# Summing the modulation's eight row tiles on VectorE instead of TensorE

## The chip, the cores and the metric

One core of one Trainium2 chip runs the whole program in one launch. The metric is the device time of an execution in microseconds (us); lower is better. PE is TensorE, DVE is VectorE, ACT is ScalarE, POOL is GpSimd, SP is SyncE, which issues most of the loads.

## What is computed

Two transformer layers on 256 context and 256 sequence tokens with 1024 features, and then a second block. Each layer first makes its modulation: shifts, scales and gates, six vectors of 1024 for each of two conditioning vectors.

```python
mod = (silu_c @ lp["w_mod"] + lp["b_mod"])[:, None, :]
sh1, sc1, gt1, sh2, sc2, gt2 = jnp.split(mod, 6, axis=-1)
n_mod_c = 6 * d if update_ctx else 2 * d
modc = (silu_cc @ lp["w_mod"][:, :n_mod_c] + lp["b_mod"][:n_mod_c])[None, None, :]
...
x = x + gt1 * merge_branches(o_mla, o_gqa, o_four, proj[..., GATE_START:], lp)
x = x + gt2 * conv_ffn(modulate(x, lp["g_norm2"], sh2, sc2), lp)
```

`w_mod` is [1024, 6144] float32 in each layer. The last layer (`update_ctx` false) uses only the first 2048 columns of the context's modulation.

## The kernel before

Products of activations and weights are made of float32 operands split into two float32r parts. `wload` (L223) loads 128 x 1024 elements of a weight on SP's queue into one of four slots `wraw`; `wsplit` (L237) makes a piece of it: ACT casts the high part `whi` (L247), DVE subtracts it to get the low part `wlo` (L249), in four slots each; then PE runs three matmuls for each pair of tiles (`mm3`, L259 to L261). With 512 tokens a piece feeds 24 such matmuls. A product's sum is held in one of five PSUM banks (`acc`) until ACT or DVE has read it.

The modulation of the first layer's first group of 2048 columns is made at the start (`first_mod`). The five other groups (two of layer 0, three of layer 1) come from the class `Mod` in 40 steps of 128 rows by 2048 columns. A step loads 1 MB of `w_mod` into a slot `mraw` (L457; two slots in the first place, three in the second) and PE multiplies it with `cT`, the conditioning vectors as 32 columns (two are used, 30 are zero), by four matmuls of 512 columns (L459) that lie on four column tiles of the array, and sums over the eight steps of a group in the PSUM bank `po`. After the eighth step `close` copies `po` to SBUF (L474), transposes it (L393) and adds the bias (L477).

The steps are traced in two places. In layer 0's remaining branches, between attention and the product with `w_o`, `mod.step(4)` stands four times between a gate's product (four pieces) and a branch's product (two pieces); the branch's operand `bhl` is split by ACT and DVE too (L378, L379), its sums are multiplied by the gate and added up on DVE (L874, L890). In layer 0's FFN, `mod.step(3)` stands after each pair of hidden tiles: a pair is four tiles of `w_up` (four pieces), each convolved by ACT and two operations of DVE on the PSUM bank (L1154, L1157), multiplied (L1205) and split (`xh`, `xl`, L379); after every second pair comes the product with `w_down`, whose sums DVE adds to the residual (L1080). The residual's gate, `hgt`, and the second norm need layer 0's two groups; layer 1 needs the other three.

What order an engine runs its instructions in is settled when the program is built: the builder moves instructions of one engine past each other where their operands allow it. At run time each engine and each DMA queue takes its own instructions in that order, and a wait holds up all behind it.

Of the kernel before, what the change touches and what calls it, by code (L numbers as in the profile page):

```python
# [10 lines left out]
F32 = mybir.dt.float32  # L11
# [26 lines left out]
def constants():  # L38
# [19 lines left out]
    # bucket of the relative position k - 255, k = 0..511 (the last one is unused)  # L58
# [24 lines left out]
class Packed:  # L83
    """A matrix [K, N], stored part by part in the order in which the program loads them; each partition's share of
    a part [k * 128 rows, c columns] is one run of k * c elements."""
# [17 lines left out]
class View:  # L103
# [8 lines left out]
    def part(self):  # L112
        """The access pattern [128, k, c] of a part that is loaded once."""
        m, n = self.m, self.shape[0] * self.shape[1]
        pos, m.pos = m.pos, m.pos + n
        assert m.pos <= m.size
        m.parts.append((pos, self.r0, self.r1, self.c0, self.c1))
        return m.ap[pos : pos + n].rearrange("(p k c) -> p k c", p=P, c=self.shape[1])


def feature_major(a):
    """[.., k * 128] as [128, .., k]"""
    a = a.reshape(*a.shape[:-1], -1, P)
    return np.moveaxis(a, -1, 0)


def setup(nc, inputs):
    """Access patterns by name, and a function that gives the arrays once the program is there."""
# [8 lines left out]
    for n in MATS:  # L137
        A[n] = []
        for l in range(i[n].shape[0]):
            a = i[n][l]  # L140
            if n == "w_br_gqa":
                # heads in the order in which the attention pairs them: one of each key head
                a = a.reshape(2, 4, 64, D).swapaxes(0, 1).reshape(512, D)
            packs.append(Packed(nc, f"{n}_{l}_dram", a, SLACK.get(n, 0)))
            A[n].append(packs[-1].view())
    put("w_mod", i["w_mod"])
    # the first layer's first shift and scale, one half of the features after the other
# [25 lines left out]
def tile_kernel(ctx: ExitStack, tc: tile.TileContext, A, C, out):  # L173
# [21 lines left out]
    # instructions that others are queued behind  # L195
# [6 lines left out]
    # PSUM banks: products and scores, transposes, attention outputs and small sums  # L202
# [19 lines left out]
    RAW = 1024  # L222

    def wload(src):
        """src: a view [k*128, cols], at most RAW elements for each partition."""
# [10 lines left out]
    def wsplit(v, into=None):  # L236
        """Parts of a piece [128, k, c] of a loaded tile, at most 1024 elements; into: a tile [128, 2, 1024]."""  # L237
# [16 lines left out]
    def hold(n):  # L254
        """The next n pieces are split behind what has been traced with to_hilo: they are ready early and would go first."""
# [7 lines left out]
    def proj_fm_steps(w, c0, ncols, act, evict, T):  # L263
        """Feature-major product: evict(ct, psum[features, T]) for each tile of 128 columns of w; a step is a tile."""
# [21 lines left out]
    def fm_half(ws, act, os_, a, ks=range(KD), n=256):  # L286
        """As proj_fm for split tiles of 128 columns and the tokens from a, a half; to be finished for both halves before
        the products in os_ are read. A step is a tile."""
# [7 lines left out]
    def tm_half(ws, n, act, tts, evict, os_=None, k=0):  # L296
        """As proj_tm for split row tiles of one window, from k, and some of the tokens. A step is a split piece."""
# [13 lines left out]
    def halves_last(ws, act, evict):  # L311
        """As proj_fm for weights that stay, all products of 256 tokens before those of the others; ws(): their split
        parts in order; evict(ct, psum, first token). A step is a tile."""
# [18 lines left out]
    def beside(work, bg, skip=0):  # L332
        """Steps of work, with one of bg after each but the first ones."""
# [4 lines left out]
    def pipeline(units, fill=None, every=1):  # L338
        """Stage j of unit i is emitted beside stage 0 of unit i + j; fill: steps of other work in between."""
# [8 lines left out]
    def proj_tm_steps(w, c0, widths, act, tts, evict):  # L348
        """Token-major product: evict(tt, window, psum[tokens, width]); a step is a split piece of w."""
# [31 lines left out]
    def rsqrt_cols(ss, n, mul, eps, name):  # L381
        """(ss * mul + eps) ** -0.5 for a [128, n] tile of sums."""
# [6 lines left out]
    def transposed(src_tiles, dst_evict, rows=P):  # L389
        """PE transposes of up to four [128, c] blocks into one PSUM bank."""  # L390
# [5 lines left out]
    # ================================================================ block 1  # L396
    # the residual, feature-major: a list of tiles [128, tokens]; its slots hold gates between its uses
# [12 lines left out]
    # silu of the two conditioning vectors, feature-major, padded to a column tile of the array  # L410
# [6 lines left out]
    # parameters by feature  # L417
# [10 lines left out]
    def after(t, x):  # L428
        """What is loaded into t comes after x."""
# [3 lines left out]
    def load_par(l):  # L433
        small.dma_start(out=par[l]["all"], in_=A["par"][l])
        small.dma_start(out=rowbc[l]["all"], in_=A["rows"][l].partition_broadcast(P))
        # the attention scales go with the queries' gains
# [6 lines left out]
    class Mod:  # L443
        """Modulation columns in groups of 2048 for both conditioning vectors, four column tiles of the array at work.
        step() does one tile of 128 rows; finish() those that are left of a group."""

        def __init__(self, src, bufs, *groups):
            self.todo, self.o, self.src, self.bufs = [], None, src, bufs
            self.todo = [(l, g, k) for l, g in groups for k in range(KD)]

        def step(self, n=1):
            for _ in range(min(n, len(self.todo))):
                l, g, k = self.todo.pop(0)
                if k == 0:
                    self.o = psum([P, 512], tag="po")
                raw = self.src.tile([P, 2048], F32, tag="mraw", name="mraw", bufs=self.bufs)
                nc.sync.dma_start(out=raw, in_=A["w_mod"][l, k * P : (k + 1) * P, g * 2048 : (g + 1) * 2048])  # L457
                for j in range(4):
                    nc.tensor.matmul(  # L459
                        self.o[32 * j : 32 * j + 32, :], cT[:, k, :], raw[:, j * 512 : (j + 1) * 512], start=(k == 0), stop=(k == KD - 1)  # L460
                    )
                if k == KD - 1:
                    self.close(l, g)
# [4 lines left out]
        def slot(self):  # L468
            """A slot of the loads' ring for a split piece."""
# [18 lines left out]
    def first_mod(h, ks=range(KD)):  # L488
        """Shift and scale of the first norm for a half of the features, four column tiles of 256 columns."""
# [3 lines left out]
        for k in ks:  # L493
            # the split weights' slots are free yet
# [24 lines left out]
    class Squares:  # L519
        """Sums of squares over feature tiles: the last tile's stay apart."""  # L520
# [5 lines left out]
        def add(self, k, a, T):  # L526
            """Feature tile k of the residual, T tokens from a."""
# [12 lines left out]
        def columns(self, o, t0, t1):  # L540
            """Sums over all features, 128 tokens to a column."""
# [5 lines left out]
    # tokens: columns 0..255 are the context's, 256..511 the sequence's  # L547
    def norm_factor(acc, t0, t1, res, tag="acc"):
        """rsqrt of the mean square over features (acc: Squares), on all partitions, in PSUM; in steps."""
# [14 lines left out]
    def norm_steps(l, which, acc, a, scaled=False, ks=range(KD), rb=None):  # L564
        """The modulated norm of 256 tokens from a, in two parts; scaled: X has been multiplied by the norm's factor."""
# [36 lines left out]
    # the first layer's residual can be read again: the tiles take the norm's factor  # L602
# [7 lines left out]
    def rope_apply(x, nh, off, half, cs):  # L610
        """Rotate x[:, :, off:off+2*half] in place; cs: [128, 4*half] = cos, cos, -sin, sin."""
# [10 lines left out]
    def head_rstd(x, nh, dh):  # L622
        """rsqrt of the mean square over each head's dims; x: [128, nh, dh]."""
# [12 lines left out]
    def layer(l):  # L636
# [31 lines left out]
        # ---- products of the input that the attentions start from  # L668
# [50 lines left out]
        # the first weights stay in slots that are taken later, for the second half of the tokens  # L719
# [9 lines left out]
        if full:  # L729
            # half of the features after the other, as their shift and scale come  # L730
# [19 lines left out]
            # fills the time that the second half's norm takes  # L750
# [20 lines left out]
        # the residual waits in DRAM, the first layer's is the input  # L771
# [10 lines left out]
        def ev_qg(tt, wi, o):  # L782
            # [j, g, d]: the four queries of a group lie side by side over the two key heads
# [28 lines left out]
        # ---- the Fourier branch; its tiles lie where the latent heads will  # L812
# [42 lines left out]
        # ---- gates that are ready before their branches: work for the array between the attentions' steps  # L855
# [13 lines left out]
        def half_tanh(dst, o):  # L869
            """sigmoid(z) = (1 + tanh(z / 2)) / 2; the last factor goes with the residual's gate."""  # L870
# [12 lines left out]
        def branch_evict(bi, gs, ct0=0):  # L883
            """y = sum over branches of (1 + tanh) * (branch @ its matrix)"""
# [22 lines left out]
        # ---- latent attention's heads  # L907
# [62 lines left out]
        # ---- attention: a unit is two heads for 128 queries  # L970
        def unit(name, tt, i, heads):
# [4 lines left out]
            def a():  # L976
                st["p"] = []
                # two heads of 64 dims lie on two row tiles of the array
# [23 lines left out]
            def c():  # L1002
# [3 lines left out]
                # the two heads on two column tiles of the array  # L1006
# [34 lines left out]
        # ---- the branches that are left  # L1041
# [6 lines left out]
        for bi, n, wn in ((1, "gqa", "w_br_gqa"), (2, "mla", "w_br_mla"))[nb - 1 :]:  # L1048
            b = load_branch((mp if full else qk).tile([P, 2, 4, T], F32R, tag="bhl" if full else "KT", name="bhl"), n)
            for dq in range(2):  # L1050
# [8 lines left out]
                if not full:  # L1059
                    # the first pieces of w_up; the context's halves of the first norm are free  # L1060
# [6 lines left out]
        # the residual returns; in the second layer only the sequence's half is of use  # L1067
# [33 lines left out]
        else:  # L1101
            # the first products of w_up go ahead of the norm's factor, which multiplies them by token:
            # (x r A + B) w = r (x A) w + B w, B as one more column
# [32 lines left out]
        # ---- FFN  # L1136
# [11 lines left out]
        def conv(u, m, name):  # L1148
            """The depthwise taps over tokens for feature tile m; u: PSUM [128, T]."""
# [13 lines left out]
        # two tiles first for the first layer, two last for the second  # L1163
# [5 lines left out]
        def pair(m0):  # L1169
            av = []  # L1170
            if full and m0 == 0:
                # the first products start with the first half of the tokens
# [50 lines left out]
        # a group's second product comes after some of the next group's first ones: its operand is ready by then  # L1223
# [661 lines left out]
```

## Time and profile before

| | us |
|---|---|
| median of 3 runs (1899.38 to 1901.94) | 1900.52 |
| span of the profiled execution | 1896.8 |
| PE busy in it | 1841.1 |
| DVE busy in it | 1265.7 |
| ACT busy in it | 933.0 |

The profiled execution has no time of its own beside its span, from the first to the last instruction. The median is 3.7 us above that span, which is what lies around it if that execution took the median time. The granted TensorE clock is 0.993 of full speed on average. A busy PE is not PE at its peak: matmuls overlap in the records, so a group's busy time is to be read together with the starts of what follows.

### The profile page before, as it was taken

The numbers are of one execution on the slowest core, as the hardware profiler recorded it, in microseconds if no ns is written. First come the engines' busy times: TensorE is split into PE (matmuls) and PEld (weight loads), VectorE is DVE, ScalarE is ACT, GpSimd is POOL, SyncE is SP. The second block draws the span as 40 slices with busy tenths as digits, with TensorE's granted clock in tenths as the row PEclk, the third lists the DMA queues.
The fourth block names the chain that finished last, engine by engine and source line by source line (L and its number), as shares of the span: only waits on it lengthen the run. The fifth ranks groups of instructions, "written<-read, shape, count | busy, mean of one in ns | idle before, by whom it ended". The sixth has DMA issues, their size and how long they took to land.

```text
span 1896.8 us, 30401 instructions
## 1 busy us (share of the span) xinstructions
PE 1841.1 (97%) x11962; PEld 1555.0 (82%) x11962; DVE 1265.7 (67%) x2317; ACT 933.0 (49%) x1561; POOL 149.9 (8%) x149
## 2 busy tenths in 40 slices
PE   6999999999999999999999999999999999999998
PEld 4788666777797777778899977999999887799996
DVE  5657776434575555456577987688787768668776
ACT  3435454223343323323445554565556647477782
POOL 0303100200120000000121200010000000200010
PEclk9999999999999999999999999999999999999999
DMA  8322210666426545422344522545565446344442
GB/s 325 114 72 77 73 62 29 205 241 222 167 79 232 178 156 211 156 89 90 108 149 149 162 83 77 195 145 188 180 192 193 160 162 201 116 145 150 156 142 98
DMA packets 86319, 281.07 MB, mean 148 GB/s; under 512 B 9616, under 2 KB 24224, under 8 KB 80288
## 3 DMA queue, kind: packets, MB, share of 16 engines
q1 hardware_dynamic: 65376, 254.91, 39.5%
q10 hardware_dynamic: 18992, 19.40, 3.2%
q0 software_dynamic: 1808, 4.82, 0.9%
q8 instruction: 94, 1.54, 0.3%
q14 instruction: 49, 0.40, 0.1%
HBM read 272.26 MB, written 8.93 MB: 148 GB/s over the span
## 4 chain that ended last, share of the span: by engine, by line
PE 88%; DVE 4%; ACT 3%; DMA 2%; issue 2%; POOL 0%; SPq 0%; ACTq 0%; DVEq 0%; POOLq 0%
PE acc L259 25%; PE acc L261 24%; PE acc L260 24%; PE acc L981 3%; PE tp L393 3%; PE po L1009 2%; PE po L459 2%; DMA mraw<-w_mod_dram 1%; PE acc L1326 1%; DVE wlo L249 1%; PE po L1354 1%; ACT whi L247 1%; DVE m L1310 0%; ACT L1432 0%; DVE scc L1270 0%
## 5 line engine op out<-in xcount | busy, mean ns | idle before, releaser
L249 DVE TENSOR_TENSOR wlo<-wraw,whi 128x1024 fp32r<-128x1024 f32 (+3 forms) x364 | 436.9, 1203 | 241.4 <-ACT whi L247 238.0
L247 ACT CAST whi<-wraw 128x1024 fp32r<-128x1024 f32 (+3 forms) x364 | 373.1, 1030 | 442.0 <-PE acc L260 352.4
L261 PE MATMUL acc<-hh,wlo 128*128 128x256 f32 (+1 forms) x1184 | 399.4, 338 | 0.0
L260 PE MATMUL acc<-hl,whi 128*128 128x256 f32 (+1 forms) x1184 | 399.1, 338 | 0.0
L259 PE MATMUL acc<-hh,whi 128*128 128x256 f32 (+1 forms) x1184 | 399.1, 338 | 0.0
L259 PEld LDWEIGHTS acc<-hh,whi 128*128 128x128 f32 x1184 | 223.4, 189 | 32.2 <-issue 4.2
L260 PEld LDWEIGHTS acc<-hl,whi 128*128 128x128 f32 x1184 | 222.9, 188 | 26.5 <-issue 2.0
L261 PEld LDWEIGHTS acc<-hh,wlo 128*128 128x128 f32 x1184 | 223.1, 189 | 24.8 <-issue 0.3
L261 PE MATMUL acc<-xh,wlo 128*128 128x256 f32 (+1 forms) x336 | 111.3, 332 | 0.0
L260 PE MATMUL acc<-xl,whi 128*128 128x256 f32 (+1 forms) x336 | 111.2, 332 | 0.0
L259 PE MATMUL acc<-xh,whi 128*128 128x256 f32 (+1 forms) x336 | 110.9, 332 | 0.0
L1080 DVE SCALAR_TENSOR_TENSOR x<-acc,mod,x 128x256 f32<-128x256 f32 x144 | 65.0, 479 | 51.5 <-PE acc L261 50.8
L538 POOL TENSOR_TENSOR nacc<-nacc,nsq 128x256 f32<-128x256 f32 x30 | 32.3, 1076 | 700.5 <-ACT nsq L533 698.7
L259 PE MATMUL acc<-h4h,whi 128*128 128x256 f32 x288 | 82.5, 287 | 1.5 <-ACT g L1432 1.5
L261 PE MATMUL acc<-h4h,wlo 128*128 128x256 f32 x288 | 81.8, 285 | 0.0
L260 PE MATMUL acc<-h4l,whi 128*128 128x256 f32 x288 | 81.6, 284 | 0.0
L259 PEld LDWEIGHTS acc<-xh,whi 128*128 128x128 f32 x336 | 63.3, 189 | 11.9 <-issue 2.5
L986 ACT ACTIVATE p<-acc,negm 128x512 f32<-128x512 f32 (+1 forms) x96 | 58.9, 621 | 27.2 <-DVE negm L984 24.1
L386 POOL TENSOR_TENSOR hr_r<-hr_t,mhalf 128x4 f32<-128x4 f32 (+2 forms) x42 | 55.3, 1318 | 193.0 <-DVE hr_t L384 189.5
L261 PEld LDWEIGHTS acc<-xh,wlo 128*128 128x128 f32 x336 | 63.5, 189 | 6.3
L260 PEld LDWEIGHTS acc<-xl,whi 128*128 128x128 f32 x336 | 63.3, 188 | 6.0
L984 DVE TENSOR_REDUCE negm<-acc 128x1 f32<-128x512 f32 (+1 forms) x96 | 56.4, 596 | 13.7 <-PE acc L981 13.1
(456 smaller groups left out, 4154.2 us busy)
## 6 DMA issues: line engine op xcount, KB each, us to landing
wraw<-w_up_dram SPq DMA_DIRECT2D x84, 512.0 KB, 3.8
mraw<-w_mod_dram SPq DMA_DIRECT2D x40, 1024.0 KB, 6.4
wraw<-w_in_dram SPq DMA_DIRECT2D x74, 512.0 KB, 3.5
wraw<-w_in_c_dram SPq DMA_DIRECT2D x60, 512.0 KB, 3.3
wraw<-w_down_dram SPq DMA_DIRECT2D x44, 512.0 KB, 3.8
wraw<-w_in_ab_dram SPq DMA_DIRECT2D x41, 512.0 KB, 4.1
mraw<-w_mod_dram SPq DMA_DIRECT2D x16, 512.0 KB, 9.8
wraw<-w_out_ab_dram SPq DMA_DIRECT2D x12, 512.0 KB, 3.7
```

The lines of the kernel that those rows point to most:

```text
L247: nc.scalar.copy(out=w(hi), in_=v)
L249: nc.vector.tensor_tensor(out=w(lo), in0=v, in1=w(hi).bitcast(F32), op=ALU.subtract)
L259: nc.tensor.matmul(o, lh, rh, start=first, stop=False)
L260: nc.tensor.matmul(o, lh, rl, start=False, stop=False)
L261: last_ops["pe"] = nc.tensor.matmul(o, ll, rh, start=False, stop=last)
L386: last_ops["pow"] = nc.gpsimd.tensor_tensor(out=r[:, :n], in0=t[:, :n], in1=mhalf[:, :n], op=ALU.pow)
L393: last_ops["tp"] = nc.tensor.transpose(o[: s.shape[1], j * P : j * P + s.shape[0]], s, ident[: s.shape[0], : s.shape[0]])
L459: nc.tensor.matmul(self.o[32 * j : 32 * j + 32, :], cT[:, k, :], raw[:, j * 512 : (j + 1) * 512], start=(k == 0), stop=(k == KD - 1))
L981: nc.tensor.matmul(S, q, k[:, :nk], start=True, stop=True)
L984: nc.vector.tensor_reduce(out=m[:, 0:1], in_=S, axis=AX.X, op=ALU.max, negate=True)
L986: nc.scalar.activation(out=p[:, :nk], in_=S, func=AF.Exp, bias=m[:, 0:1], scale=1.0, accum_out=m[:, 1:2])
L1080: nc.vector.scalar_tensor_tensor(out=X[ct][:, a : a + 256], in0=o[:, a - t0 : a - t0 + 256], scalar=gate[:, ct, w : w + 1], in1=X[ct][:, a ...
```

## The change

A step no longer uses PE. For each conditioning vector `v` it multiplies the loaded tile by that vector's column of `cT`, one number for each partition, and adds it to an accumulator `macc` of 128 x 2048 in SBUF, in two halves of 1024: one `tensor_scalar` for a half in a group's first step, one `scalar_tensor_tensor` in the seven others, all on DVE. After the eighth step PE sums each accumulator over the partitions into `po`, by four matmuls whose stationary operand `pick` is 32 columns with ones in column `v` and zeros elsewhere. In layer 1's second and third groups only the sequence's vector is made. The accumulators take 16 KB more of each partition in both places. Comments were removed too; what stands in the diff is all else.

```diff
+    pick = const1("pick", [P, 2, 32])
+    nc.vector.memset(pick, 0.0)
+    for v in range(2):
+        nc.vector.memset(pick[:, v, v : v + 1], 1.0)
...
         def step(self, n=1):
             for _ in range(min(n, len(self.todo))):
                 l, g, k = self.todo.pop(0)
+                vs = range(1 if l and g else 2)
                 if k == 0:
-                    self.o = psum([P, 512], tag="po")
+                    self.acc = [self.src.tile([P, 2048], F32, tag=f"macc{v}", name="macc") for v in vs]
                 raw = self.src.tile([P, 2048], F32, tag="mraw", name="mraw", bufs=self.bufs)
                 nc.sync.dma_start(out=raw, in_=A["w_mod"][l, k * P : (k + 1) * P, g * 2048 : (g + 1) * 2048])
-                for j in range(4):
-                    nc.tensor.matmul(
-                        self.o[32 * j : 32 * j + 32, :], cT[:, k, :], raw[:, j * 512 : (j + 1) * 512], start=(k == 0), stop=(k == KD - 1)
-                    )
+                for v in vs:
+                    for s in (slice(0, 1024), slice(1024, 2048)):
+                        a, c = self.acc[v][:, s], cT[:, k, v : v + 1]
+                        if k == 0:
+                            nc.vector.tensor_scalar(out=a, in0=raw[:, s], scalar1=c, scalar2=None, op0=ALU.mult)
+                        else:
+                            nc.vector.scalar_tensor_tensor(out=a, in0=raw[:, s], scalar=c, in1=a, op0=ALU.mult, op1=ALU.add)
                 if k == KD - 1:
+                    o = psum([P, 512], tag="po")
+                    for v in vs:
+                        for j in range(4):
+                            nc.tensor.matmul(
+                                o[32 * j : 32 * j + 32, :], pick[:, v], self.acc[v][:, j * 512 : (j + 1) * 512], start=(v == 0), stop=(v == vs[-1])
+                            )
+                    self.o = o
                     self.close(l, g)
```

The builder moves other instructions with it. In the changed program line numbers below `Mod` are 18 higher (L1154 is L1172, L1205 is L1223, L874 is L892). Three places:

PE, at the end of the first gate's product in the branches (`hh` is the norm's output, `bhl` the branch's operand, `po` the bank of the modulation). Before, here after two steps:

```order
L261 MATMUL acc<-hh,wlo 128x512
L459 MATMUL po<-mraw,cT 32x512 x8
L259 MATMUL acc<-bhl,whi 128x512
L260 MATMUL acc<-bhl,whi 128x512
L261 MATMUL acc<-bhl,wlo 128x512
```

Now, where the first group ends, after the second gate's product:

```order
L261 MATMUL acc<-hh,wlo 128x512
L477 MATMUL po<-macc,pick 32x512 x2
L259 MATMUL acc<-bhl,whi 128x512
L260 MATMUL acc<-bhl,whi 128x512
L477 MATMUL po<-macc,pick 32x512 x2
L261 MATMUL acc<-bhl,wlo 128x512
L259 MATMUL acc<-bhl,whi 128x512
L260 MATMUL acc<-bhl,whi 128x512
```

No matmul of a step is left; a group's eight come in four pairs here, with matmuls of the branch between them.

DVE, from the last of some parameters' operations (`nq`) on, in the branches. Before:

```order
L1849 TENSOR_SCALAR nq<-omlb 128x12
L249 TENSOR_TENSOR wlo<-wraw,whi 128x1024
L379 TENSOR_TENSOR bhl<-braw,bhl 128x512
L249 TENSOR_TENSOR wlo<-wraw,whi 128x1024
L379 TENSOR_TENSOR bhl<-braw,bhl 128x512 x3
L249 TENSOR_TENSOR wlo<-wraw,whi 128x1024
L874 SCALAR_TENSOR_TENSOR gate<-gate,acc 128x512
L890 TENSOR_TENSOR gt_1339<-gt_1339,gate 128x512
L874 SCALAR_TENSOR_TENSOR gate<-gate,acc 128x512
L890 TENSOR_TENSOR gt_1340<-gt_1340,gate 128x512
```

Now:

```order
L1867 TENSOR_SCALAR nq<-omlb 128x12
L470 TENSOR_SCALAR macc<-mraw,cT 128x1024 x4
L472 SCALAR_TENSOR_TENSOR macc<-mraw,cT,macc 128x1024 x4
L249 TENSOR_TENSOR wlo<-wraw,whi 128x1024
L472 SCALAR_TENSOR_TENSOR macc<-mraw,cT,macc 128x1024 x7
L249 TENSOR_TENSOR wlo<-wraw,whi 128x1024
L379 TENSOR_TENSOR bhl<-braw,bhl 128x512
L472 SCALAR_TENSOR_TENSOR macc<-mraw,cT,macc 128x1024
L379 TENSOR_TENSOR bhl<-braw,bhl 128x512
L249 TENSOR_TENSOR wlo<-wraw,whi 128x1024
L379 TENSOR_TENSOR bhl<-braw,bhl 128x512 x2
L472 SCALAR_TENSOR_TENSOR macc<-mraw,cT,macc 128x1024 x7
```

The branch's operand was split beside the next two pieces; 15 operations of the modulation now stand ahead of its first split, and one more ahead of the second.

DVE in the FFN, from the first hidden tile's multiplication on (`cv` are convolved tiles, `xh` and `xl` the split hidden tile). Before:

```order
L1205 TENSOR_TENSOR cv<-cv 128x512
L1154 SCALAR_TENSOR_TENSOR cv<-acc,par_99,cv 128x2x255
L1157 SCALAR_TENSOR_TENSOR cv<-acc,par_99,cv 128x2x255
L379 TENSOR_TENSOR xl<-cv,xh 128x512
L1205 TENSOR_TENSOR cv<-cv 128x512
L379 TENSOR_TENSOR xl<-cv,xh 128x512
L249 TENSOR_TENSOR wlo<-wraw,whi 128x512
L1154 SCALAR_TENSOR_TENSOR cv<-acc,par_99,cv 128x2x255
```

Now:

```order
L1223 TENSOR_TENSOR cv<-cv 128x512
L470 TENSOR_SCALAR macc<-mraw,cT 128x1024 x4
L1172 SCALAR_TENSOR_TENSOR cv<-acc,par_103,cv 128x2x255
L379 TENSOR_TENSOR xl<-cv,xh 128x512
L472 SCALAR_TENSOR_TENSOR macc<-mraw,cT,macc 128x1024 x4
L1175 SCALAR_TENSOR_TENSOR cv<-acc,par_103,cv 128x2x255
L249 TENSOR_TENSOR wlo<-wraw,whi 128x512
L472 SCALAR_TENSOR_TENSOR macc<-mraw,cT,macc 128x1024
L1172 SCALAR_TENSOR_TENSOR cv<-acc,par_103,cv 128x2x255
L472 SCALAR_TENSOR_TENSOR macc<-mraw,cT,macc 128x1024 x3
L1223 TENSOR_TENSOR cv<-cv 128x512
L249 TENSOR_TENSOR wlo<-wraw,whi 128x512
```

The second hidden tile's multiplication came soon after the first's, with its split `xl` right behind it. Now twelve of the modulation's operations stand between the two multiplications, four more and three convolution operations between the second one and its split, and a tile's second convolution operation no longer follows its first at once.

## Rows read from the trace of the kernel before

**Rows 1.** The page's first part: busy time, share of the span, instructions

```profile
PE 1841.1 (97%) x11962; PEld 1555.0 (82%) x11962; DVE 1265.7 (67%) x2317; ACT 933.0 (49%) x1561; POOL 149.9 (8%) x149
```

**Rows 2.** The page's chain that ended last, by engine

```profile
PE 88%; DVE 4%; ACT 3%; DMA 2%; issue 2%; POOL 0%; SPq 0%; ACTq 0%; DVEq 0%; POOLq 0%
```

**Rows 3.** Stages by window: us, PE, PEld, DVE, ACT, POOL busy, PEclk, DMA share, GB/s

```profile
340.00:500.00 160.00, 157.89 (x755) 113.77 (x753) 59.95 (x90) 41.74 (x58) 10.67 (x21) 1.00 0.63 222
580.00:820.00 240.00, 240.00 (x1114) 176.94 (x1113) 130.03 (x183) 79.45 (x101) 0.00 (x0) 1.00 0.50 181
```

**Rows 4.** The same windows, line 459's instructions alone: us, PE, PEld, PEclk

```profile
340.00:500.00 160.00, 16.22 (x128) 2.93 (x128) 1.00 0.63 222
580.00:820.00 240.00, 25.17 (x192) 5.26 (x192) 1.00 0.50 181
```

**Rows 5.** PE in order of time: start, us, line, tiles, count, idle before

```profile
367.17 0.40 PE L261 MATMUL acc<-hh,wlo 128*128 128x512 f32 x1
367.50 1.93 PE L459 MATMUL po<-mraw,cT 128*32 128x512 f32 x16
369.35 0.50 PE L259 MATMUL acc<-bhl,whi 128*128 128x512 f32 x1
...
379.23 1.07 PE L459 MATMUL po<-mraw,cT 128*32 128x512 f32 x8 [1.45 <-DMA mraw<-w_mod_dram]
```

**Rows 6.** The chain that ended last, in order of time, FFN of layer 0

```profile
605.16 2.71 PE po L459 x24
...
615.06 0.97 PE po L459 x2
```

**Rows 7.** Tile mraw: time to landing of its loads

```profile
DMA to landing us min/median/max: 4.8/7.0/13.7
```

**Rows 8.** PE's waits, 340 to 830 us: total, times, longest

```profile
PE po L459 <- DMA mraw<-w_mod_dram: 2.1, 2, 1.4
PE acc L259 <- ACT whi L247: 1.7, 2, 1.3
```

**Rows 9.** DVE groups by form: count, busy us, mean ns

```profile
L249 DVE TENSOR_TENSOR wlo<-wraw,whi 128x1024 fp32r<-128x1024 f32 x347 | 424.6, 1227 | 227.8 <-ACT whi L247 224.7 <-PE tp L393 1.7 <-PE acc L261 0.2
...
L993 DVE TENSOR_SCALAR p<-p,negm 128x512 f32<-128x512 f32 x64 | 30.8, 482 | 1.5
...
L993 DVE TENSOR_SCALAR p<-p,negm 128x256 f32<-128x256 f32 x32 | 10.7, 346 | 0.2
...
L1769 DVE SCALAR_TENSOR_TENSOR ke<-g,ke 128x1024 f32<-128x1024 f32 x6 | 7.3, 1209 | 0.0
```

**Rows 10.** DVE in order of time, the branches and w_o

```profile
353.33 0.17 DVE L1849 TENSOR_SCALAR nq<-omlb 128x12 f32<-128x12 f32 x1
...
501.23 2.36 DVE L249 TENSOR_TENSOR wlo<-woraw,whi 128x1024 fp32r<-128x1024 f32 x2
```

**Rows 11.** DVE in order of time, the first pairs of the FFN

```profile
581.17 0.74 DVE L1154 SCALAR_TENSOR_TENSOR cv<-acc,par,cv 128x510 f32<-128x510 f32 x1
581.95 0.75 DVE L1157 SCALAR_TENSOR_TENSOR cv<-acc,par,cv 128x510 f32<-128x510 f32 x1
582.62 0.68 DVE L379 TENSOR_TENSOR xl<-cv,xh 128x512 fp32r<-128x512 f32 x1
583.21 0.69 DVE L1205 TENSOR_TENSOR cv<-cv 128x512 f32<-128x512 f32 x1
...
689.55 0.88 DVE L1080 SCALAR_TENSOR_TENSOR x<-acc,mod,x 128x256 f32<-128x256 f32 x2 [1.92 <-PE acc L261]
```

**Rows 12.** PE in order of time, where the second pair's products begin

```profile
579.34 0.39 PE L260 MATMUL acc<-hl,whi 128*128 128x512 f32 x1
579.57 0.39 PE L261 MATMUL acc<-hh,wlo 128*128 128x512 f32 x1
```

**Rows 13.** The chain that ended last, in order of time, branches of layer 0

```profile
369.48 13.70 DMA mraw<-w_mod_dram
```

More of the change, by code (lines that the diff above doesn't have):

```diff
@@ L447, in __init__ @@
         def __init__(self, src, bufs, *groups):
-            self.todo, self.o, self.src, self.bufs = [], None, src, bufs
+            self.todo, self.acc, self.src, self.bufs = [], None, src, bufs
             self.todo = [(l, g, k) for l, g in groups for k in range(KD)]
```

## Prediction

> **What bounds the kernel now.** I read the page's busy times first: PE is busy for 97% of the span and DVE for 67% [rows 1]. The chain of waits that ended last agrees: 88% of it is PE, 4% DVE [rows 2]. So PE time that goes away should shorten the run, as long as no other engine becomes late. Whether one does must be read where the steps stand, since 67% is a mean over stages. The windows show two such places: the branches, 340 to 500 us, with PE at 157.9 and DVE at 60.0 of 160; and the FFN, 580 to 820 us, with PE at 240.0 and DVE at 130.0 of 240 [rows 3]. DVE is half idle in both, and that is what the change draws on.
>
> **What goes from PE.** Line 459 is busy 16.2 us in the branches and 25.2 in the FFN [rows 4], 41.4 in all. Not all of it holds up PE: a set of four matmuls is 1.07 us busy, but the next matmul starts earlier. In time order two sets take 1.93 us, from 367.50, and the next product starts at 369.35 [rows 5]; in the chain three sets take 2.71 [rows 6]. I take off 0.07 us for each of the 26 stretches in which the steps stand (12 and 14): 15.4 + 24.2 = 39.6 us. PE also waited for the loads of these steps, 2.1 us in two waits, one of them the 1.45 in the timeline [rows 5, 8], and 1.7 us for ACT's first splits of `w_o` [rows 8]. Two of `w_o`'s four loads use the modulation's slots, which now come free before the last branch instead of behind PE; I take that wait off too. Removed: 43.4 us.
>
> **What PE gets back.** 32 `pick` matmuls, of the same shape as line 459's: eight for each of three groups, four for each of two. A set of four side by side costs 0.90 to 1.0 us, but a lone one costs 0.97 too [rows 6], because what runs beside it is missing. So count visits. The first group's four pairs lie apart: 4 x 0.97 = 3.9. The second group has six together and two apart: 1.87 + 0.97 = 2.8. The FFN's groups have eight together (1.85), one and three (1.94), and four (0.97): 4.8. Sum 11.5 us. Copy, transposes and bias after a group stay as they were. With nothing else late, PE's path is shorter by 43.4 - 11.5 = 31.9 us.
>
> **What DVE gets.** 24 steps with four operations and 16 with two: 128, of which 16 are `tensor_scalar` and 112 `scalar_tensor_tensor`, 64 in each place. One of the second kind on 128 x 1024 takes 1209 ns in block 2, a split of that size 1227 [rows 9]. Back to back two splits take 2.36 us [rows 10], so one adds 1.14. `tensor_scalar` is there at 512 and 256 columns, 482 and 346 ns; 1024 would be 482 + 2 x 136 = 754, 0.69 back to back (my estimate). Added: 112 x 1.14 + 16 x 0.69 = 139 us, 69.4 in each place.
>
> The Trainium skill ("VectorE: DVE Perf Modes", section "The DRAIN you can't avoid") says that the next operation doesn't start until the pipe has emptied. The row disagrees for operations that wait for nothing: two in 2.36 us, not in 2 x 1.22 [rows 10]. By that rule the 112 would cost some 8 us more, and the forecast below, by the same share of stalls, some 1 us more.
>
> So DVE would be busy 129 us of about 148 in the branches and 199 of about 220 in the FFN (each window less what PE sheds): 87% and 90%. On average there is room. But DVE takes its queue in order, and what PE needs stands behind the new operations: low parts of pieces (three or four pieces, some 16 us, ahead of PE, so seldom missed), the branch's operand, and the reads that free PSUM banks (five). I follow the two places that the order shows, with the prices above, 0.6 us for an operation of 512 columns, 0.78 for one of the convolution and 0.84 for a pair on the residual [rows 11].
>
> *Branches.* DVE is done with `nq` at 353.5 [rows 10]. Four scalings (2.8), four sums (4.6) and a split end at 362.0. The third tile's load can start when the first slot is free, 356.3; it takes 7.0 [rows 7] and lands at 363.3. Four sums, three on the fourth tile, a split and the first split of `bhl` end at 373.0. PE comes for that split when the gate's product ends, 367.5 [rows 5] (the order puts four matmuls first that don't need it): it stands from 368.4 to 373.0, **4.6 us**. It then has 22 matmuls of 0.23 us to run, and the other three splits are there by 377. Later DVE keeps up: its work through the second group ends about when PE comes for it.
>
> *FFN.* After the first multiplication DVE is at 581.2 [rows 11]. To the second hidden tile's split the order has four scalings, twelve sums, six convolution operations and six of 512 columns: 2.8 + 13.7 + 4.7 + 3.6 = 24.8, to 606.0. PE begins the second pair just before 579.34 [rows 12] and has 96 matmuls, 22.4 us, to 601.6; eight of `w_down`'s need no such split; it stands from 603.5 to 606.0, 2.5. Then banks: the fourth `w_down` tile needs the bank of the second pair's third tile, whose last convolution operation comes at 613.4, and the fifth that of the fourth, at 620.1; PE is there at 608.2 and 614.8. That is 5.2 + 5.3 more, **13 us** in all. In the two later groups a step has only two operations, mostly one between two reads of banks, and the tally finds DVE late but no wait.
>
> **Sum.** 31.9 - 18 = 14 us. The profiled execution is 1896.8 us of span, the median 3.7 above it, so 1886.6: **1887 us**.
>
> **The bounds.** No row prices a stall of this kind. From below it is 0: DVE has idle time enough in total; that gives 1868.6. From above I take the FFN's first group, 13 us for 32 operations, 0.41 us each, for all 128: 52 us, and 1920. My 18 us are 0.14 for each operation; at 0.25 the gain is gone. I keep near my tally because the other three quarters of the operations stand farther apart, or meet operands made long before.
>
> **Rivals.**
> - *DVE's idle time covers it.* Stalls of under 8 us; near 1872. For: the tally lets the builder's order of reads decide at single microseconds, and PE runs 16 us behind its pieces. Against: the order puts the branch's operand and the banks behind 12 to 17 operations.
> - *The gain is eaten.* Stalls of 27 to 36 us: 1896 to 1904. DVE is at 90% in both places, and my tally gives it no wait for ACT's part of a split or for a load over 7 us; one load took 13.7 in the branches [rows 13], beside traffic that remains. Four loads in a row that are 6.7 us over the median would put DVE 27 us behind, with pieces for 16 us ahead.
> - *Slower: DVE becomes the bound.* The banks of the FFN are freed late in every group, not in the first alone, at 0.41 us for each operation; 1920. It decides from 0.28, 36 us of stalls. Against: later groups have half the operations for each step, and DVE has some 20 us of idle time left there.
>
> **Chances.** Forecast (stalls of 8 to 27 us) 0.47, covered 0.22, eaten 0.18, slower 0.13. A measurement tells this kernel from no change from about 0.2%, 3.8 us: 1896.7 to 1904.3. Eaten is nearly that band; I count a sixth of it as just under. So faster 0.72, same 0.15, slower 0.13. The range leaves out the slowest rival and little of the covered case: 1869 to 1902.
>
> **What would show it.** In the profile of the changed kernel: line 459 gone and 32 `pick` matmuls (64 records) of some 12 us; 112 sums at about 1.21 us and 16 scalings at about 0.75; PE idle before `acc<-bhl` at the first branch, released by DVE's `bhl`, about 5 us; PE idle in the first `w_down` product, released by DVE (`xl`, then convolution), about 13; DVE busy 139 us more; no PE wait for `mraw`. I am wrong if PE stands for DVE in many other places too, if sums cost clearly more than 1.2 us, or if DVE itself waits long for `mraw`.

## The result and the profile after

The changed kernel takes **1879.11 us** (median of 4 runs, 1878.41 to 1880.04) against 1899.95 before (4 runs on the same chip, 1897.66 to 1901.94). The ratio is 0.9892, with a 95% interval of [0.9879, 0.9905]: faster by 1.1%. The forecast was 1887, in a range of 1869 to 1902. Direction and mechanism held; the gain was 20.8 us where about 14 was forecast. The span of the profiled execution went from 1896.8 to 1876.6, 20.2 us less, and it is those 20.2 that the traces have to account for.

The page of the changed kernel: busy time by engine, then the chain by engine, then the group of the new sums (count | busy us, mean ns | idle before). They answer to [rows 1], [rows 2] and [rows 9].

```profile
PE 1814.6 (97%) x11706; PEld 1552.6 (83%) x11706; DVE 1400.2 (75%) x2448; ACT 931.3 (50%) x1561; POOL 150.3 (8%) x149
...
PE 85%; DVE 7%; ACT 3%; issue 2%; DMA 2%; POOL 0%; SPq 0%; ACTq 0%; DVEq 0%
...
L472 DVE SCALAR_TENSOR_TENSOR macc<-mraw,cT,macc 128x1024 f32<-128x1024 f32 x112 | 139.8, 1284 | 3.5 <-DMA mraw<-w_mod_dram 3.5
```

PE is still the bound, but DVE's part of the chain grew from 4% to 7%: PE now waits for it. DVE is 134.5 us busier, forecast 139. A sum takes 1284 ns where 1209 was taken. It waited for a load of its own once, 3.5 us.

The same two windows as [rows 3], columns as there, after the change:

```profile
340.00:500.00 160.00, 156.47 (x717) 120.40 (x716) 134.82 (x163) 46.18 (x63) 10.68 (x21) 0.99 0.70 240
580.00:820.00 240.00, 231.49 (x1002) 182.45 (x1001) 195.36 (x252) 79.64 (x101) 0.00 (x0) 0.99 0.52 176
```

The `pick` matmuls alone in these windows (us, PE, PEld, clock), answering to [rows 4]:

```profile
340.00:500.00 160.00, 7.17 (x32) 1.11 (x32) 0.99 0.70 240
580.00:820.00 240.00, 5.09 (x32) 0.86 (x32) 0.99 0.52 176
```

41.4 us of PE time became 12.3. In the FFN's window PE, which had no gap at all before, now stands for 8.5 us of 240. PE's waits from 340 to 830 us in the changed kernel (total, times, longest) show for what; they answer to [rows 8]:

```profile
PE acc L259 <- DVE cv L1175: 4.8, 1, 4.8
PE acc L260 <- DVE bhl L379: 3.5, 1, 3.5
...
PE acc L259 <- DVE x L1098: 3.0, 1, 3.0
PE acc L260 <- DVE xl L379: 0.7, 1, 0.7
```

The waits for `mraw` and for ACT's first splits of `w_o` are gone, as forecast. Four waits for DVE have come, 12.0 us: the branch's operand, and in the FFN a split, a bank and a residual tile. Where the three of the FFN lie, first on PE (start, us, line, tiles, count, idle before):

```profile
595.21 0.50 PE L260 MATMUL acc<-xl,whi 128*128 128x512 f32 x1 [0.74 <-DVE xl L379]
...
597.40 0.40 PE L261 MATMUL acc<-xh,wlo 128*128 128x512 f32 x1
602.57 0.80 PE L259 MATMUL acc<-xh,whi 128*128 128x512 f32 x1 [4.77 <-DVE cv L1175]
603.16 0.63 PE L260 MATMUL acc<-xl,whi 128*128 128x512 f32 x1
603.59 0.63 PE L261 MATMUL acc<-xh,wlo 128*128 128x512 f32 x1
...
605.66 0.39 PE L260 MATMUL acc<-xl,whi 128*128 128x512 f32 x1
605.89 0.39 PE L261 MATMUL acc<-xh,wlo 128*128 128x512 f32 x1
...
614.17 0.47 PE L259 MATMUL acc<-hh,whi 128*128 128x512 f32 x1 [3.00 <-DVE x L1098]
```

and on DVE, which hasn't one idle moment there:

```profile
599.37 2.49 DVE L472 SCALAR_TENSOR_TENSOR macc<-mraw,cT,macc 128x1024 f32<-128x1024 f32 x2
601.75 0.76 DVE L1175 SCALAR_TENSOR_TENSOR cv<-acc,par,cv 128x510 f32<-128x510 f32 x1
...
611.94 1.30 DVE L472 SCALAR_TENSOR_TENSOR macc<-mraw,cT,macc 128x1024 f32<-128x1024 f32 x1
613.13 0.89 DVE L1098 SCALAR_TENSOR_TENSOR x<-acc,mod,x 128x256 f32<-128x256 f32 x2
```

The convolution that frees PE's bank starts the moment two sums end. They don't need PE, and PE needs what stands behind them. After the wait matmuls follow each other at 0.43 us, from 605.66 on again at 0.23: a cost that the waits don't list.

### The profile page after: what moved, and what is told of

Its sections match the earlier page's. It is cut to its first block, busy times and chain, and to the rows that moved or that the text cites. A ratio compares the mean times of both kernels' runs of the same rounds, so it can differ in the third digit from the quotient of the medians.

```text
span 1876.6 us, 30048 instructions
## 1 busy us (share of the span) xinstructions
PE 1814.6 (97%) x11706; PEld 1552.6 (83%) x11706; DVE 1400.2 (75%) x2448; ACT 931.3 (50%) x1561; POOL 150.3 (8%) x149
## 4 chain that ended last, share of the span: by engine, by line
PE 85%; DVE 7%; ACT 3%; issue 2%; DMA 2%; POOL 0%; SPq 0%; ACTq 0%; DVEq 0%
PE acc L259 24%; PE acc L261 24%; PE acc L260 24%; PE acc L999 3%; PE tp L393 3%; PE po L1027 2%; DVE wlo L249 1%; PE acc L1344 1%; PE po L1372 1%; DVE macc L472 1%; ACT whi L247 1%; DMA mraw<-w_mod_dram 1%; PE po L477 1%; DMA braw<-drgqa 1%; DVE scc L1288 0%
## 5 line engine op out<-in xcount | busy, mean ns | idle before, releaser
L472 DVE SCALAR_TENSOR_TENSOR macc<-mraw,cT,macc 128x1024 f32<-128x1024 f32 x112 | 139.8, 1284 | 3.5 <-DMA mraw<-w_mod_dram 3.5
```

Of the source, the lines that this page charges most:

```text
L472: nc.vector.scalar_tensor_tensor(out=a, in0=raw[:, s], scalar=c, in1=a, op0=ALU.mult, op1=ALU.add)
```

## Experiments

The theory: PE's time is worth what the trace says, and what the change gives back is waits that come from *where* the new operations stand in DVE's queue. Rivals: the gain is that of loads; or DVE is simply too full. Some of the expectations below call the second rival their theory; the text says which one each result fits. The runs come from several chips, on which the kernel before has medians from 1899.07 to 1901.07, so a difference of a microsecond or two between two rows of the table is not read; the ratio is always to the kernel before on the same chip.

| run | median us | ratio to before, 95% |
|---|---|---|
| the change | 1879.1 | 0.9892 [0.9879, 0.9905] |
| branches alone | 1889.3 | 0.9946 [0.9934, 0.9959] |
| FFN alone | 1887.9 | 0.9938 [0.9924, 0.9951] |
| a quarter of the steps, on PE | 1862.4 | 0.9798 [0.9783, 0.9813] |
| one pair later | 1878.9 | 0.9886 [0.9872, 0.9900] |
| one vector | 1871.8 | 0.9843 [0.9829, 0.9856] |
| even | 1878.6 | 0.9884 [0.9871, 0.9897] |
| behind the first branch | 1886.7 | 0.9921 [0.9908, 0.9935] |
| two vectors everywhere | 1886.2 | 0.9926 [0.9913, 0.9938] |
| even, behind `xl` | 1871.8 | 0.9862 [0.9847, 0.9878] |
| behind `bhl` | 1881.2 | 0.9908 [0.9891, 0.9925] |
| both orders | 1878.2 | 0.9888 [0.9873, 0.9904] |
| even, behind `xl`, picks together | **1864.0** | 0.9809 [0.9795, 0.9822] |

### One place at a time

```diff
...
+                if l == 1:
+                    if k == 0:
+                        self.o = psum([P, 512], tag="po")
+                    for j in range(4):
+                        nc.tensor.matmul(self.o[32 * j : 32 * j + 32, :], cT[:, k, :], ...)
+                    ...
+                    continue
                 for v in vs:
```

> The first layer's groups are summed on DVE, the FFN's three groups on PE as before the change. Theory (PE's time is worth what it says, less picks and the waits that DVE's order makes): 15.4 us of step matmuls and 3.8 of waits for mraw and w_o go, 7.2 of picks and a 3.5 us stall at bhl come: 8.5 us faster, about 1891.5; no PE wait for DVE after 580 us. Rival (the gain is that of loads, the matmuls' time was hidden): the 3.8 us alone less the stall, so no gain, 1899 to 1900. Rival (DVE's load in one place makes it late in the other): this and the run with the FFN alone together gain clearly more than the change's 20.8, 25 or more.

The other run has `l == 0` there.

> The FFN's three groups are summed on DVE, the first layer's two on PE as before the change. Theory: 24.2 us of step matmuls go, 5.1 of picks and 8.5 of stalls (xl, a bank, a residual tile) come: 10.6 us faster, about 1889.3, with the three stalls where the changed kernel has them. Rival (loads): no gain, since PE waited for no load of these steps: 1899 to 1905. Both places then add up to 19 to 21 us by the theory; 25 or more if one place's load harms the other.

Measured: 9.8 and 11.2 us faster than the kernel before. Together that is 21.0, and both at once gave 20.8, so the two places don't harm each other. The stall at `bhl` is there when the branches alone are changed; PE's waits of that run:

```profile
...
PE acc L260 <- DVE bhl L379: 3.3, 1, 3.3
PE acc L259 <- DVE gate L902: 1.3, 1, 1.3
```

With the FFN alone PE's waits for DVE there are 6.5 us, in other shares (3.3 for convolutions, 3.2 for residual tiles; another 1.2, for `ab`, come at 501 us, ahead of it). The rival of the loads falls: the FFN had no wait for a load to lose, and gained 11.2.

### A quarter of the matmuls, nothing for DVE

```diff
-                for j in range(4):
+                for j in range(4 if k in (0, KD - 1) else 0):
```

> The kernel before, with all loads, but only the first and the last of a group's eight steps multiplied: six eighths of the modulation's sum are left out, so this bounds what PE's time is worth with nothing given to DVE. Theory: 40 sets become 10, most of them lone at 0.97 us: PE sheds about 30 us, and between none and all of the 3.8 us of waits: 1866 to 1870. Rival (loads): the matmuls' time is hidden behind loads or DVE; less than half of it shows, 1885 or more.

Measured: 1862.4, 36.6 us less, more than the 30 to 34 expected. In the window of 340 to 840 us PE has no wait left but 3.4 us for `ndiag` (3.9 before). Of 36.2 us of span 4.3 are waits, so 30 sets are worth 32 us, 1.06 each. I had taken 0.99. A reason is seen at the visit of four lone matmuls below.

### The steps moved in the program, not in the queue

```diff
-            mod.step(3)
+            mod.step(0 if m0 == 0 else 3 if m0 < 10 else 4)
```

> The changed kernel, with the FFN's steps starting behind the second pair instead of the first (3 a pair, then 4 for the last three pairs). Theory (it is the place in DVE's queue that makes the stalls, the first group's 32 operations beside the first two down products): the 8.5 us of stalls and some of the clock's dip behind them go, 1869 to 1873. Rival (DVE is simply too full in the FFN with two vectors): the stalls move with the steps, by the next pair's products; 1877 to 1882. In between if one of the three goes.

```diff
-            mod.step(3)
+            mod.step(2 if m0 < 8 else 4)
```

> The changed kernel with the FFN's 24 steps spread so that each pair has eight operations: two steps (two vectors) behind each of the first four pairs, four (one vector) behind each of the last four. Nothing is left out. Theory (DVE is full only where 12 operations stand in a pair): 16 + 9.7 of 30 us everywhere, the 8.5 us of stalls mostly go: 1868 to 1873. Rival (the moved steps meet other waits, as when they came one pair later): 1876 to 1880.

Measured: 1878.9 and 1878.6, no change, with the same 4.8 us wait for the convolution. The first lies in the range of a DVE that is too full, the second in that of moved steps that meet other waits. The trace says why neither result counts. DVE in order of time in the run with even steps:

```profile
601.15 2.47 DVE L472 SCALAR_TENSOR_TENSOR macc<-mraw,cT,macc 128x1024 f32<-128x1024 f32 x2
603.54 0.74 DVE L1175 SCALAR_TENSOR_TENSOR cv<-acc,par,cv 128x510 f32<-128x510 f32 x1
```

The same two sums stand ahead of the same convolution as in the changed kernel at 599.37. Nothing in the program ties a sum to its pair: it needs a loaded tile, and the builder, which orders DVE's queue, moved the sums of the later calls forward into the same places: from 565 to 640 us the modulation keeps DVE busy for 38.7 us in the changed kernel and for 37.5 and 37.6 in these two. These two runs tried nothing, and no verdict rests on them. The next went the same way:

```diff
-                mod.step(4)
+                mod.step((0, 5, 5, 6)[2 * (bi - 1) + dq])
```

> The changed kernel with the first layer's 16 steps as 0, 5, 5 and 6 instead of 4 each: none before the first branch's product, so that its operand's split isn't behind them. Theory: the 3.5 us stall at bhl and the dip of the clock behind it go, nothing else changes: 1874 to 1876. Rival (DVE gets too full later in the branches, 20 to 24 operations in a stretch): other stalls of 3 us or more, in the second branch or at w_o's first pieces, 1877 to 1883.

Measured: 1886.7, 7.6 slower than the change and above both ranges. PE's waits from 340 to 840 us:

```profile
...
PE acc L260 <- DVE bhl L379: 3.6, 1, 3.6
PE po L477 <- DVE macc L472: 3.6, 1, 3.6
...
PE acc L259 <- ACT whi L247: 2.6, 2, 2.1
```

The wait at `bhl` stayed, and the end of the last group came late: the picks waited for its sums, and `w_o`'s first splits are late again. The profile that was taken has a span of 1880.0, so some 5 us of the median aren't in it. The four other executions have a lower granted clock (0.986 to 0.989, against 0.991 in the profiled one); where it was low, no trace shows.

### Fewer and more operations

```diff
-                vs = range(1 if l and g else 2)
+                vs = range(1 if l else 2)
```

> The changed kernel, but the FFN's first group too is summed for one vector only (the context's modulation of the next layer's first norm is left out): 16 operations less on DVE, four pick matmuls less. Theory (DVE is full for the length of that group: a pair's 30 us have some 16 us of other DVE work and 12 operations of 1.2): with 6 a pair the 8.5 us of FFN stalls and the clock's dip behind them go, 0.9 of picks too: 1867 to 1871. Rival (the place in the queue alone decides): a stall or two of 3 to 5 us stays, 1873 to 1878.

Measured: 1871.8, and PE's waits there are

```profile
PE acc L260 <- DVE bhl L379: 3.8, 1, 3.8
...
PE acc L259 <- DVE x L1098: 1.4, 2, 1.1
```

so with 16 operations less in the FFN's first group 7.1 of the 8.5 us went, and no stall of 3 to 5 us stayed there. The time lies just above the 1867 to 1871 of a DVE that is too full and under the 1873 to 1878 of the place alone: taken by itself, this run speaks for the number of operations. The other side:

```diff
-                vs = range(1 if l and g else 2)
+                vs = range(2)
```

> The changed kernel, but the FFN's two later groups are summed for both vectors as well (the context's, which nobody reads): 32 operations more on DVE (some 38 us) and eight pick matmuls (some 2 us). Theory: every pair then asks DVE for some 30.7 of 30 us; FFN stalls grow from 8.5 to 20 to 30 us: 1892 to 1904. Rival (the first group's stalls are its place beside the first two down products): only the picks show, and a stall or two, 1881 to 1886.

Measured: 1886.2, 7.0 slower than the change, under the 1892 to 1904 of a DVE that is too full and at the upper edge of its rival, the place. PE's waits in the FFN are 10.5 us instead of 8.5:

```profile
PE acc L259 <- DVE cv L1175: 5.3, 2, 4.8
PE acc L259 <- DVE x L1098: 3.8, 2, 2.0
...
PE acc L260 <- DVE xl L379: 1.4, 1, 1.4
```

So 32 operations more in the later groups cost 2 us of waits, 0.06 us each, and not the 0.41 of my slower rival, although there are as many for a pair there now as in the first group. The eight added picks are 1.7 us. The rest goes with the clock: in the first pairs, where this run has the operations of the changed kernel, the granted clock is 0.89 from 580 to 610 us and 0.94 from 610 to 640, where the changed kernel has 0.94 and 1.00. The run with even steps has 0.89 and 0.94 there too, so this isn't a price of the added operations. A full DVE doesn't by itself make stalls. In the changed kernel it is busy without a gap from 640 to 670 us, and PE has no gap either (columns as in [rows 3]):

```profile
640.00:655.00 15.00, 15.00 (x69) 12.08 (x68) 15.00 (x20) 4.70 (x6) 0.00 (x0) 1.00 0.88 298
655.00:670.00 15.00, 15.00 (x66) 12.08 (x65) 15.00 (x19) 5.74 (x8) 0.00 (x0) 1.00 0.89 310
```

What sets the first group apart is what stands behind its sums.

### The same operations in another place in the queue

Two steps behind each of the first four pairs, four behind the others, and an edge that keeps DVE's operations of a step behind the last `xl` of the pair traced before:

```diff
+                        with tc.issue_after(last_ops["dve"].ins) if l == 1 else ExitStack():
                             if k == 0:
                                 nc.vector.tensor_scalar(out=a, in0=raw[:, s], scalar1=c, ...)
...
-            mod.step(3)
+            mod.step(2 if m0 < 8 else 4)
```

> The changed kernel with the FFN's steps two behind each of the first four pairs and four behind each of the last, and each step's DVE operations now ordered behind the low part of the pair's second hidden tile (without such an edge the builder had moved them ahead of it again). Same operations, same number. Theory (the stalls come from where these operations stand in DVE's in-order queue, ahead of reads that free PE's banks): the 8.5 us of FFN stalls and the clock's dip behind them go: 1868 to 1872, bhl's 3.5 stays. Rival (DVE is too full for 32 operations beside the first pairs, wherever they stand): stalls of 5 us or more stay, 1875 to 1880.

Measured: 1871.8. DVE in order of time there (lines are one higher):

```profile
579.13 3.66 DVE L473 SCALAR_TENSOR_TENSOR macc<-mraw,cT,macc 128x1024 f32<-128x1024 f32 x3
582.72 0.74 DVE L1176 SCALAR_TENSOR_TENSOR cv<-acc,par,cv 128x510 f32<-128x510 f32 x1
...
593.98 0.73 DVE L1176 SCALAR_TENSOR_TENSOR cv<-acc,par,cv 128x510 f32<-128x510 f32 x1
...
598.72 0.68 DVE L379 TENSOR_TENSOR xl<-cv,xh 128x512 fp32r<-128x512 f32 x1
599.32 4.86 DVE L473 SCALAR_TENSOR_TENSOR macc<-mraw,cT,macc 128x1024 f32<-128x1024 f32 x4
```

No sum stands between 582.72 and 599.32, where the banks come due, and four in a row stand where nothing does. The stretch as a whole, columns as in [rows 3]:

```profile
580.00:610.00 30.00, 30.00 (x130) 24.32 (x130) 27.18 (x40) 12.23 (x16) 0.00 (x0) 1.00 0.44 157
610.00:640.00 30.00, 30.00 (x130) 24.31 (x130) 26.16 (x30) 11.45 (x15) 0.00 (x0) 1.00 0.46 158
```

DVE is 27.2 and 26.2 of 30 us busy, 89%, and PE has no gap. All 8.5 us of FFN waits are gone, and over the whole FFN there is not one operation less. But the run changed two things: beside the place, the modulation's operations between 565 and 640 us, which keep DVE busy for 23.2 us here and for 38.7 in the changed kernel. That their place alone, with as many of them beside the first two pairs, would do it isn't shown: steps of three with the edge were not run. What speaks for place is that DVE can be full without a stall of PE, as above, and the branches, next, where only the order was changed and the wait moved with it.

The same for the branches, the first group behind the four splits of `bhl` (the condition is `(l, g) == (0, 1)`, the steps are the changed kernel's), and then both:

> The changed kernel with the first layer's first group (eight steps) ordered on DVE behind the four splits of the first branch's operand bhl. Theory: the 3.5 us stall there goes with some 1.5 us of lowered clock behind it; the FFN's 8.5 stay: 1873 to 1876. Rival: the group is done later, and its picks, the second group or w_o's first splits wait instead: 1877 to 1882.

> Both orders together. Theory: all 12 us of waits for DVE between 340 and 840 us go, and the clock's dips: 1862 to 1868, near the bound that the run with a quarter of the matmuls gave (1862). Rival (the waits move): 1870 or more.

Measured: 1881.2 and 1878.2; the rival held. PE's waits from 340 to 840 us with the branches' order alone:

```profile
...
PE acc L259 <- ACT bhl L378: 3.4, 1, 3.4
PE acc L260 <- DVE xl L379: 1.8, 1, 1.8
PE acc L259 <- ACT whi L247: 1.7, 3, 0.9
PE tp L393 <- ACT modrow L493: 0.7, 1, 0.7
...
```

The first branch's wait is gone. But the group is done later, and `hgt`, which is made from it, comes at 442.2 us instead of 430.2; the second branch's operand is late in its place (3.4 at 443.06), and the first of `w_o`'s loads starts at 484.0 instead of 461.8, as its slots are the modulation's, so the wait that the change had removed is back. The 3.5 us at `bhl` were the price of an early group. With both orders the FFN's waits are gone as well, but PE's waits from 340 to 840 us are 8.3 us against 6.6 with the FFN's order alone; the rest of the 6.3 us between these two runs isn't placed.

### Lone picks and picks together

```diff
+                    first = None
+                    for v in reversed(vs):
+                        for j in reversed(range(4)):
+                            with tc.issue_after(first.ins) if first else ExitStack():
+                                mm = nc.tensor.matmul(o[32 * j : 32 * j + 32, :], pick[:, v], ..., start=(v == vs[-1]), stop=(v == 0))
+                            first = first or mm
```

> The run with two, then four, steps behind each pair (1871.8), with a group's pick matmuls ordered behind the one that needs the last half of the last sum, so that they come together: 6 visits of PE instead of 14. Same operations. Theory (a visit costs about 0.97 us whether it has two or four column tiles, eight together 1.9): picks take about 7.7 us instead of about 15, so some 6 to 8 us faster, 1864 to 1866. Rival (lone picks overlap with the products around them, their busy time isn't PE's path): 1870 to 1873. Rival (the group's end comes later and something waits for it): a new wait of 1 us or more in front of the transposes, hgt or the next group's scalings.

Measured: **1864.0**, 36.9 us under the kernel before on the same chip. It beats both kernels. A lone visit, in PE's order of time of the run without this edit:

```profile
406.42 0.39 PE L260 MATMUL acc<-bhl,whi 128*128 128x512 f32 x1
406.74 1.05 PE L478 MATMUL po<-macc,pick 128*32 128x512 f32 x4
407.72 0.50 PE L261 MATMUL acc<-bhl,wlo 128*128 128x512 f32 x1
408.06 0.39 PE L259 MATMUL acc<-bhl,whi 128*128 128x512 f32 x1
```

and eight together with it:

```profile
411.62 0.40 PE L259 MATMUL acc<-bhl,whi 128*128 128x512 f32 x1
411.95 1.92 PE L480 MATMUL po<-macc,pick 128*32 128x512 f32 x16
413.80 0.50 PE L260 MATMUL acc<-bhl,whi 128*128 128x512 f32 x1
414.14 0.39 PE L261 MATMUL acc<-bhl,wlo 128*128 128x512 f32 x1
```

Two picks take 0.98 us to the next product, eight take 1.85. And each visit costs at its edges: the product before it lasts 0.32 to 0.33 and the one behind it 0.34, where products otherwise follow at 0.23. So a lone visit costs 1.64 - 2 x 0.23 = 1.18 us here, and eight together 2.52 - 0.46 = 2.06. With eight visits fewer, picks are 8.1 us busy instead of 15.6, and the run is 7.8 us faster.

## Why the prediction was right

**What goes from PE** was right in kind and too small. The 39.6 us came from taking something off for each stretch of steps; the edges say that 0.13 is to be added. 41.4 + 26 x 0.13 = 44.8. With the waits of 3.8, which went as forecast, and 0.5 less at `ndiag`, 49.1.

**What PE gets back**: 11.5 forecast. The same edges on the same visits: four and one lone ones in the branches, with six together; in the FFN eight together and three lone ones. That is 8 x 1.18 + 2 x 2.06 = 13.6.

**The stalls** are the term that was mis-sized: 18 forecast, 12.0 measured. At the branch's split it was 3.5 for 4.6: DVE was to stand 1.3 us for the third tile's load, and in the trace its seven sums run without a gap. In the FFN the tally of DVE's queue was good. From the first multiplication to the end of the second tile's split it gave 24.8 us, and the trace has 24.6 (570.5 to 595.1); to the bank's last reader 32.2, and 31.9 (to 602.4). The first two waits together, 7.7 forecast and 5.5 measured, are short mostly because DVE began earlier against PE: 0.4 us behind the second pair's first matmul (570.13), where the prediction's times have 2.0. The step that failed is the last one: "the fifth that of the fourth", 5.3 us. After 602.57 PE ran five `w_down` tiles in a row without waiting; its next wait was the following pair's first tile, 3.0 us for a residual tile. So that tile didn't need the bank that I had given it.

**What was missing** is the slow clock behind a wait, priced below at 2.7 us in this trace.

**The sum by what was measured**: 49.1 - 13.6 - 12.0 - 2.7 = 20.8, against 20.2 us of span. Stalls account for 6 of the 7 us by which the forecast missed; the edges add 3.1, `ndiag` 0.5, and the clock takes 2.7. That the edges and the clock, neither of them in the forecast, nearly cancel is luck.

The time that was forecast has one more fault: it put 3.7 us around the profiled span. Each execution that lists both has 1.8 between them (1878.41 and 1876.6), so the other 1.9 were the distance of the profiled execution from the median, and the same sum would have given 1884.7.

**Durations**: scaling 749 ns (754 forecast), sums 1284 (1209). Back to back four sums take 4.87 us, 1.20 each. That cost nothing that shows, as the FFN's tally came out.

The Trainium skill ("VectorE: DVE Perf Modes", section "The DRAIN you can't avoid") says that the next operation doesn't start until the pipe has emptied, and adds, which the prediction left out, "A next op that is not held starts earlier." The trace agrees with the addition: the sums start 1.20 us apart at 1.28 each.

**The rivals.** "Covered" needed stalls under 8 us, and the change has 12; with the sums spread and ordered behind `xl` it comes true (1871.8). "Eaten" and "slower" rested on a load or a full DVE. DVE waited 3.5 us for a load, once, without an effect seen on PE, and 32 operations more cost 0.06 us each of waits, not 0.41.

## What to carry to other kernels

Moving work from a full engine to a half idle one is worth the full engine's time, edges of each visit included, less what the receiver's queue then delays; look in that queue for what stands directly ahead of the reads that free banks. Where a builder orders the queue, moving a call in the program may move nothing: tie the work with an edge to the operation it should stand behind, read the new order, and check what else is fed by the work you delay. Many-in-one forms (four column tiles side by side) pay only if they arrive together.

## What had not been expected of the hardware

After two of the waits PE's clock fell. The window of 374 to 378 us, 1.8 us behind the end of the 3.53 us wait at `bhl`, has a granted clock of 0.64 in the changed kernel:

```profile
374.00:378.00 4.00, 4.00 (x14) 3.10 (x13) 4.00 (x5) 0.00 (x0) 0.00 (x0) 0.64 1.02 250
```

Matmuls of 512 columns follow at 0.23 us first, from 373.80 to 376.79 at 0.43, the level of 1.2 GHz, then at 0.23 again, that of 2.4. Behind the 4.77 us wait the low level is there at once, from 602.57 to 605.29 (granted clock 0.50): six matmuls in 2.7 us, 1.3 more than at the full level. Two such stretches make the 2.7 us of the sum. Behind the waits of 0.74 and 3.00 us the pitch stayed at its level. The length of a wait doesn't decide alone: with the branches alone the pitch stayed behind a wait of 3.34 us at `bhl`, and with even steps it fell behind one of 2.36 us, 12 us after another of 4.77.

A `scalar_tensor_tensor` of 1024 columns took 1284 ns with its factor from a tile and 1209 with a constant [rows 9]. The factor may be the reason; the two also differ in their operators, and no run tried either alone.
